# Attention with the values as the moving operand: one over the row sum applied to a token-major output that is transposed afterwards, and the statistics of the first projections taken after the third

## The chip, the core and the metric

The kernel runs on one core of a Trainium2 chip. The core has a matrix engine (TensorE, PE in the profile; its weight loads are the row PEld), VectorE (DVE), ScalarE (ACT), GpSimd (POOL) and SyncE (SP), which issues most DMAs. The engines run side by side, each through its own instructions in a fixed order, and wait for each other by semaphores. The metric is the device time of one execution in microseconds; the median of several runs counts.

## The reference, cut to what matters

A two-layer encoder over 1024 tokens of width 1024, float32. Layer 0 is a pair of recurrent mixers, layer 1 is softmax attention in chunks; each layer ends with an MLP and a gated embedding. The change lies in layer 1, whose attention is

```python
def chunk_band_attention(h, w_qkv, q_g, k_g, rel_bias):
    qkv = (h @ w_qkv).reshape(bsz, seq, 3, C_HEADS, C_HEAD_DIM)      # 16 heads x 64
    q = rmsnorm(qkv[:, :, 0], q_g) * (C_HEAD_DIM ** -0.5)
    k = rmsnorm(qkv[:, :, 1], k_g)
    v = qkv[:, :, 2]
    ...
    def one_chunk(c):                                                # CHUNK = 64, the chunk and 8 before it
        s = jnp.einsum('bqhd,bkhd->bhqk', q_c, k_b).astype(jnp.float32) + bias
        s = jnp.where(valid, s, -jnp.inf)
        prob = jax.nn.softmax(s, -1).astype(v.dtype)
        return jnp.einsum('bhqk,bkhd->bqhd', prob, v_b)
```

where h is the RMS-normalised residual, and the result goes through the output projection `attn_w_out`.

## The kernel before

**Staging.** Matrix products are made in two float32r parts, a rounded high part and the rest, so that one float32 product is three matmuls (high x high, high x low, low x high); where one operand isn't split, two. Layer 1's attention walks 16 steps s: 8 pairs of heads `pr` times two halves `hf` of the tokens. Four generators share PE: two `attn_lane`s, `attn_norms` and `attn_ins`. `Trunk.run` picks the next one to go on: it keeps a planned time `now`, which `mm` and `tr` move on by a planned length, and a yield with a name delays its generator by the figure for it in the table `LAT`; of those whose time has come, the first in the list goes on, so that the projections of `attn_ins` fill what the lanes leave. Behind that, the framework's scheduler sets each engine's final order and the semaphores, from the dependencies between tiles.

**Projections.** `attn_in` makes, for 128 tokens at a time, a group of 24 matmuls of 128x384 (q, k and v of a pair of heads) in a bank of the two-deep pool `dps`. ACT and DVE evacuate it to `qk` and `vs` with the scale `rscol`, one over the root mean square of the token. For the first pair of heads `rscol` is made by `row_stats` behind the first group: eight matmuls against ones over `accs`, which GpSimd sums in layer 0's tail (L1627), then a chain of small DVE operations (L375, L286 to L291). `load_qkv` brings the weights of the next pair: three pieces `wraw` by DMA, each split by ACT (L1824) and DVE (L1825). `attn_norm` transposes q and k (`dps<-ident,qk`) and normalises them.

**One job** (`attn_block`) is 256 queries, two groups of 128, of one head. For each group the scores of up to five blocks of 128 keys are made in the PSUM tiles `sn` (near keys) and `sf` (far keys); DVE adds the relative bias and takes the maximum; ACT takes the exponential into `pb` with its sum in `l` (L1967, L1970); DVE adds the sums and takes the reciprocal (L1972, L1973); ACT multiplies `pb` by it (L1974). Then PE transposes the blocks of `pb` into `pt`, ACT and DVE split them into `ptile` (L349, L350), and PE makes the output in `po`: the key block's values `vs` are stationary and the transposed probabilities of up to 256 queries move past. `vs` holds, in 128 columns, the high part of a head's 64 columns and the low part beside it, so half of `po`'s partitions hold the product with the one and half that with the other. After a head's second job ACT copies one half (L2015, `otmp`) and DVE adds the other (L2016, `y`). `y` is head-major, and after the second head it is written to DRAM for the output projection; for the last step it is split straight into `ylast`. `po` is one bank, shared by the two jobs of a head, and the next head waits until it is read.

The order that the change touches: a job's value product waits in the plan for that of the job before (`("pv", job - 1)`), and a step's projections for the step three before to be done (`("at", s - 3)`).

## Time and profile before

| | us |
|---|---|
| median of 3 runs (3086.08 to 3091.52) | 3089.84 |
| the profiled execution | 3089.73 |
| its span, first to last instruction | 3088.0 |
| the attention stage in it, 1691 to 2308 | 617 |
| PE busy in that stage | 567.78 |
| ACT busy in that stage | 433.73 |
| DVE busy in that stage | 427.33 |

The profile is of one execution. A row of a group gives the line, the engine and operation, out<-in by the program's names, the shape and count, the busy time, the mean length of one in ns, and the idle time of the engine ahead of it with what ended it. A row of a stretch gives its bounds, its length, and the busy time of each engine with its instructions, the granted clock of PE, the share of the DMA engines and GB/s. A row of the timeline gives start and length in us. Matmuls follow each other faster than one takes, so their pace is read from the starts.

### The profile page before, as it was taken

What the parts mean: (1) busy time and instruction counts of PE and PEld (TensorE: products, weight loads), DVE (VectorE), ACT (ScalarE), POOL (GpSimd) and SP (SyncE); (2) the same over time, 40 slices, a digit from 0 to 9 for tenths busy, and PEclk for the clock granted to TensorE, in tenths of its full rate; (3) what the DMA queues carried; (4) which work ended last, traced back from release to release, by engine and by line L of the source; (5) the groups of instructions that cost most, each with busy time, mean ns of one, the idle gap of its engine ahead of it and who ended that gap; (6) DMA issues with size and microseconds to landing.
All of it is one profiled execution on the core that took longest, in us unless ns stands there. A gap on an engine that the chain in (4) does not pass through costs nothing.

```text
span 3088.0 us, 47130 instructions
## 1 busy us (share of the span) xinstructions
PE 2979.5 (96%) x17288; PEld 2461.2 (80%) x17288; DVE 2232.1 (72%) x4518; ACT 1510.7 (49%) x2922; POOL 544.9 (18%) x978
## 2 busy tenths in 40 slices
PE   7999999999999999999999999989899999999999
PEld 5777778777777888888887988888788888888887
DVE  6656676657849788878867666766768888888762
ACT  4333443334427544444434577777756544544431
POOL 6533442443500000000015111100110000000002
PEclk9999999999999999999999999999999999999999
DMA  4211112211346434754424101100256444754432
GB/s 138 72 54 62 55 55 74 62 53 64 125 158 219 158 148 150 259 167 150 137 89 144 34 33 36 53 33 16 72 177 225 151 154 150 255 172 150 126 109 102
DMA packets 187639, 358.45 MB, mean 116 GB/s; under 512 B 45712, under 2 KB 47888, under 8 KB 187408
## 3 DMA queue, kind: packets, MB, share of 16 engines
q1 hardware_dynamic: 158608, 303.00, 29.6%
q10 hardware_dynamic: 28800, 52.44, 4.4%
q8 instruction: 136, 2.23, 0.3%
...
## 4 chain that ended last, share of the span: by engine, by line
PE 79%; DVE 10%; ACT 4%; DMA 3%; POOL 2%; issue 2%; SPq 0%; DVEq 0%; POOLq 0%; ACTq 0%
PE dps L177 66%; PE ch L177 2%; PE pm L177 2%; PE iz L177 1%; PE po L177 1%; PE tp L177 1%; DVE ptile L350 1%; PE pt L192 1%; DVE pb L1957 1%; PE sn L177 1%; POOL subt L415 1%; PE py L177 1%; DMA wraw<-in_w_qkv 1%; ACT pb L1970 1%; POOL sub L417 1%
## 5 line engine op out<-in xcount | busy, mean ns | idle before, releaser
L177 PE MATMUL dps<-r,act 128*128 128x512 f32 x3528 | 829.4, 392 | 0.0
L177 PEld LDWEIGHTS dps<-r,act 128*128 128x128 f32 x3528 | 662.0, 188 | 145.8
L177 PE MATMUL dps<-xg,whi 128*128 128x512 f32 x1280 | 434.0, 419 | 14.9 <-ACT xg L352 7.4
L1614 POOL TENSOR_TENSOR pn<-pn,prs 128x512 f32<-128x512 f32 x32 | 47.1, 1474 | 1543.1 <-ACT prs L386 1447.7
L177 PE MATMUL dps<-wq,act 128*128 128x384 f32 x1536 | 305.7, 345 | 6.4 <-DVE vs L1866 3.1
L177 PEld LDWEIGHTS dps<-xg,whi 128*128 128x128 f32 x1280 | 233.9, 195 | 67.9 <-issue 8.0
L177 PEld LDWEIGHTS dps<-wq,act 128*128 128x128 f32 x1536 | 266.6, 191 | 10.5 <-DVE vs L1866 4.9
L177 PE MATMUL dps<-xg,wlo 128*128 128x512 f32 x640 | 258.8, 405 | 1.3 <-DVE wlo L304 1.3
L177 PE MATMUL dps<-late,act 128*128 128x512 f32 x960 | 229.2, 392 | 0.0
L177 PEld LDWEIGHTS dps<-late,act 128*128 128x128 f32 x960 | 180.3, 188 | 39.7
L1271 ACT CAST act<-act 128x512 fp32r<-128x512 f32 (+1 forms) x223 | 137.6, 649 | 131.6 <-PE dps L177 67.5
L1384 DVE TENSOR_TENSOR late<-late,dps 128x512 f32<-128x512 f32 x224 | 152.4, 684 | 52.2 <-PE dps L177 45.8
L1271 ACT CAST act<-late 128x512 fp32r<-128x512 f32 x210 | 124.2, 617 | 133.2 <-PE dps L177 90.4
L177 PE MATMUL dps<-act 128*128 128x512 f32 x672 | 165.0, 392 | 0.0
L1272 DVE TENSOR_TENSOR act<-act 128x512 fp32r<-128x512 f32 (+1 forms) x223 | 154.8, 721 | 6.0 <-ACT act L1271 5.8
L177 PEld LDWEIGHTS dps<-act 128*128 128x128 f32 x672 | 126.1, 188 | 28.7
L1272 DVE TENSOR_TENSOR act<-late,act 128x512 fp32r<-128x512 f32 x210 | 141.5, 688 | 8.9 <-ACT act L1271 7.0
L177 PEld LDWEIGHTS dps<-xg,wlo 128*128 128x128 f32 x640 | 124.4, 194 | 29.2 <-DVE wlo L304 1.8
L303 ACT CAST whi<-wraw 128x1024 fp32r<-128x1024 f32 x78 | 81.9, 1050 | 122.0 <-PE dps L177 82.4
L1522 DVE TENSOR_TENSOR xw<-xw,dps 128x512 f32<-128x512 f32 x174 | 118.0, 683 | 31.5 <-PE dps L177 31.5
L177 PE MATMUL dps<-xw,act 128*128 128x512 f32 x576 | 139.6, 392 | 0.0
L1389 ACT ACTIVATE late<-late 128x512 f32<-128x512 f32 x128 | 80.3, 630 | 119.4 <-DVE late L1384 113.5
...
## 6 DMA issues: line engine op xcount, KB each, us to landing
...
```

What stands on the lines that cost most here:

```text
L177: return self.begin(self.nc.tensor.matmul(out, lhsT, rhs, start=start, stop=stop, skip_group_check=again))
L192: return self.begin(self.nc.tensor.transpose(out, in_, ident))
L303: nc.scalar.copy(hi, raw)
L350: nc.vector.tensor_tensor(dst[:, 1, sl], src, dst[:, 0, sl].bitcast(F32), op=ALU.subtract)
L415: E.tensor_tensor(o, X[:, 0:i, i:i + 1].broadcast_to((NP, i, n)), Bq[:, i:i + 1, i + 1:16].broadcast_to((NP, i, n)), op=ALU.mult)
L417: E.tensor_tensor(X[:, 0:i, i + 1:16], X[:, 0:i, i + 1:16], o, op=ALU.add)
L1271: A.copy(hi, s)
L1272: V.tensor_tensor(lo, s, hi.bitcast(F32), op=ALU.subtract)
L1384: V.tensor_tensor(r, t, u, op=ALU.add)
L1389: A.activation(t, t, AF.Relu)
L1522: V.tensor_tensor(x[n][:, hs[hf]], x[n][:, hs[hf]], ps, op=ALU.add)
L1614: G.tensor_tensor(pn, pn, prs[:, sl], op=ALU.mult)
```

## The change

Per group of 128 queries, the transposed probabilities (`ptile`) are now stationary and the values `vs` move past, so `po` is token-major: for a group, 128 tokens by the 64 columns of the high part and the 64 of the low. A job that made 12 matmuls (8 of 256 columns, 4 of 128; fewer near the start) makes 20 of 128. The pass L1974 over `pb` is gone; one over the sum is applied when a group's output is evacuated: ACT copies the high half times it into the token-major `y`, DVE adds the low half times it (L2021 and L2022 of the new kernel). After the second head's second job, and a new yield `attn_block4`, PE transposes the four token groups of `y` into a `pt` bank, and ACT copies that to the tile that goes to DRAM, or the split for `ylast` reads it. `l` gets eight buffers for four, since it is read later.

For the first pair of heads the first two projection groups go to the two `sn` banks and the third to a `dps` bank; `row_stats` runs behind the third, in a `pt` bank, and the three are evacuated after it.

In the table, `attn_block1` goes from 4.45 to 3.60 and `attn_block4` is new at 0.75.

```diff
--- before.py
+++ after.py
@@ -84,9 +84,10 @@
     "gdn_back4": 1.83,
     "attn_norm0": 0.24,
     "attn_block0": 0.97,
-    "attn_block1": 4.45,
+    "attn_block1": 3.60,
     "attn_block2": 0.43,
     "attn_block3": 0.94,
+    "attn_block4": 0.75,
     "qk": 11.25,
     "norm": 1.28,
     "end_front": 46.33,
@@ -363,11 +364,11 @@
             nc.scalar.activation(sq, src, AF.Square)
             nc.gpsimd.tensor_tensor(acc, acc, sq, op=ALU.add)
 
-    def row_stats(self, accs, out, scale=1.0 / D, eps=1e-6):
+    def row_stats(self, accs, out, scale=1.0 / D, eps=1e-6, bank=None):
 
         nc = self.nc
         nt = out.shape[-1]
-        ps = self.stat_bank()
+        ps = bank if bank is not None else self.stat_bank()
         for i in range(nt):
             self.mm(ps[:, i:i + 1], accs[i // 4][:, (i % 4) * P:(i % 4 + 1) * P], self.ones[:, 0:1],
                              start=True, stop=True)
@@ -1844,9 +1845,21 @@
         qk = wp.tile([P, 4, 256], F32, tag="qk", name="qk")
         vs = l1.tile([P, 4, 2, P], F32R, tag="vs", name="vs", bufs=4)
         kv["vs"] = kv["vs"] + [vs]
+        def scale(i, e, ps):
+            rc = self.rscol[:, i:i + 1]
+            A.activation(qk[:, e, :], ps[:, 0:2, :].rearrange("p a c -> p (a c)"), AF.Copy, scale=rc)
+            v3 = ps[:, 2, :].rearrange("p (h d) -> p h d", h=2)
+            vf = vs[:, e].rearrange("p h c -> p (h c)").rearrange("p (q d) -> p q d", d=64)
+            hi = vf[:, 0:4:3, :]
+            A.activation(hi, v3, AF.Copy, scale=rc)
+            V.scalar_tensor_tensor(vf[:, 1:3, :], v3, rc, hi.bitcast(F32), op0=ALU.mult, op1=ALU.subtract)
+        held = []
         for e in range(4):
             i = 4 * hf + e
-            ps = self.bank([P, 3, P])
+            if pr == 0 and i < 2:
+                ps = psm.tile([P, HB], F32, tag="sn", name="dps", bufs=2)[:, 0:3 * P].rearrange("p (a c) -> p a c", a=3)
+            else:
+                ps = self.bank([P, 3, P])
             ts = slice(i * P, i * P + P)
             for k in range(NK):
                 ks = slice(k * P, k * P + P)
@@ -1855,15 +1868,13 @@
                 self.mm(ps, xh, wl[:, :, ks], start=False, stop=False)
                 self.mm(ps, xl, wh[:, :, ks], start=False, stop=k == NK - 1)
                 yield 0
-            if pr == 0 and i == 0:
-                self.row_stats(self.accs, self.rscol)
-            rc = self.rscol[:, i:i + 1]
-            A.activation(qk[:, e, :], ps[:, 0:2, :].rearrange("p a c -> p (a c)"), AF.Copy, scale=rc)
-            v3 = ps[:, 2, :].rearrange("p (h d) -> p h d", h=2)
-            vf = vs[:, e].rearrange("p h c -> p (h c)").rearrange("p (q d) -> p q d", d=64)
-            hi = vf[:, 0:4:3, :]
-            A.activation(hi, v3, AF.Copy, scale=rc)
-            V.scalar_tensor_tensor(vf[:, 1:3, :], v3, rc, hi.bitcast(F32), op0=ALU.mult, op1=ALU.subtract)
+            held.append((i, e, ps))
+            if pr == 0 and i == 2:
+                self.row_stats(self.accs, self.rscol, bank=psm.tile([P, HB], F32, tag="pt", name="st", bufs=2))
+            if pr or i > 1:
+                for h in held:
+                    scale(*h)
+                held.clear()
             yield 0
         q4 = qk.rearrange("p i c -> p (i c)").rearrange("p (n d) -> p n d", d=64)
         ss = self.sm.tile([P, 16], F32, tag="ss1", name="ss1")
@@ -1914,7 +1925,6 @@
             t = st["toep"][h]
             G.tensor_scalar(t, t, rbl[:, 2 * pr + h:2 * pr + h + 1], None, op0=ALU.subtract)
             G.memset(t[0:64, 320:384], NEG)
-        hs = slice(64 * h, 64 * h + 64)
         Q, Ql, K, vs, toep = st["Q"], st["Ql"], st["K"], st["vs"], st["toep"][h]
 
         def score(ps, m, j0, n):
@@ -1956,7 +1966,7 @@
             S = pb[:, nf * P:(nf + nn) * P]
             V.tensor_tensor_reduce(S, pn[:, 0:nn * P], toep[:, (3 - nn) * P:], op0=ALU.add, op1=ALU.max,
                                    scale=1.0, scalar=NEG, accum_out=mx[:, 0:1])
-            l = sm.tile([P, 4], F32, tag="l", name="l", bufs=4)
+            l = sm.tile([P, 4], F32, tag="l", name="l", bufs=8)
             if nf:
                 pf = psm.tile([P, HB], F32, tag="sf", name="sf")
                 score(pf[:, 0:nf * P], m, f0, nf)
@@ -1971,8 +1981,7 @@
             if nf:
                 V.tensor_tensor(l[:, 0:1], l[:, 0:1], l[:, 1:2], op=ALU.add)
             V.reciprocal(l[:, 2:3], l[:, 0:1])
-            A.activation(pb[:, 0:(nf + nn) * P], pb[:, 0:(nf + nn) * P], AF.Copy, scale=l[:, 2:3])
-            probs.append((pb, f0))
+            probs.append((pb, f0, l[:, 2:3]))
             yield "attn_block0"
         yield "attn_block1"
 
@@ -1981,7 +1990,7 @@
             yield ("pv", job - 1)
         if blk == 0:
             st["po", h] = psm.tile([P, HB], F32, tag="o", name="po")
-        po = st["po", h][:, 256 * blk:256 * blk + 256]
+        po = st["po", h].rearrange("p (m c) -> p m c", m=4)[:, 2 * blk:2 * blk + 2]
         pts = []
         for b in range(bank + 1):
             pt = psm.tile([P, HB], F32, tag="pt", name="pt", bufs=2)
@@ -1990,7 +1999,7 @@
                     continue
                 for e in range(2):
                     if c0 <= 128 * e < c1:
-                        pb, f0 = probs[e]
+                        pb, f0, _ = probs[e]
                         self.tr(pt[:, o + 128 * e - c0:o + 128 * e - c0 + P],
                                             pb[:, (j - f0) * P:(j - f0 + 1) * P], self.ident)
             t = self.wp.tile([P, 2, HB], F32R, tag="ptile", name="ptile", bufs=3)
@@ -1998,31 +2007,33 @@
             pts.append(t)
             yield "attn_block2"
         yield "attn_block3"
-        nmm = 2 * len(segs)
-        q = 0
-        for j, c0, c1 in segs:
-            b, o, _, _ = place[j]
-            for part in range(2):
-                self.mm(po[:, c0:c1], vs[j // 4][:, j % 4, h, :], pts[b][:, part, o:o + c1 - c0],
-                                 start=q == 0, stop=q == nmm - 1)
-                q += 1
-        if blk == 1:
-            if h == 0:
-                st["y"] = l1.tile([P, HB], F32, tag="y", name="y", bufs=1)
-            y, po = st["y"], st["po", h]
-            oth = slice(64 * (1 - h), 64 * (1 - h) + 64)
-            tmp = l1.tile([P, HB], F32, tag="otmp", name="otmp", bufs=1)
-            A.copy(tmp[hs], po[oth])
-            V.tensor_tensor(y[hs], po[hs], tmp[hs], op=ALU.add)
-            if h == 1:
-                if s == 15:
-                    yield ("ylast", 0)
-                    self.split_scaled(self.ylast, y, None, slice(0, HB))
-                else:
-                    nc.sync.dma_start(out=self.yd[pr][hf], in_=y)
-                self.dump("y1", y, (pr, slice(None), slice(hf * HB, hf * HB + HB)))
-                self.mark(("at", s))
+        if h == 0 and blk == 0:
+            st["y"] = l1.tile([P, 4, 2, 64], F32, tag="y", name="y", bufs=1)
+        for e in range(2):
+            js = [j for j, c0, c1 in segs if c0 <= 128 * e < c1]
+            for j in js:
+                b, o, c0, _ = place[j]
+                o += 128 * e - c0
+                for part in range(2):
+                    self.mm(po[:, e, :], pts[b][:, part, o:o + P], vs[j // 4][:, j % 4, h, :],
+                            start=j == js[0] and part == 0, stop=j == js[-1] and part == 1)
+            y, rl = st["y"][:, 2 * blk + e, h, :], probs[e][2]
+            A.activation(y, po[:, e, 0:64], AF.Copy, scale=rl)
+            V.scalar_tensor_tensor(y, po[:, e, 64:128], rl, y, op0=ALU.mult, op1=ALU.add)
         self.mark(("pv", job))
+        if h == 1 and blk == 1:
+            yield "attn_block4"
+            pt = psm.tile([P, HB], F32, tag="pt", name="pt", bufs=2)
+            for e in range(4):
+                self.tr(pt[:, e * P:(e + 1) * P], st["y"][:, e].rearrange("p h d -> p (h d)"), self.ident)
+            if s == 15:
+                yield ("ylast", 0)
+                self.split_scaled(self.ylast, pt, None, slice(0, HB))
+            else:
+                yt = l1.tile([P, HB], F32, tag="otmp", name="yt", bufs=1)
+                A.copy(yt, pt)
+                nc.sync.dma_start(out=self.yd[pr][hf], in_=yt)
+            self.mark(("at", s))
```

What this makes of the order. First PE, in the middle of the stage: one job's value product before, with the transposes of `pb` around it. A row with waits names the engine whose semaphore it waits for.

```order
L177 MATMUL po<-ptile,vs 128x256 [waits Activation_49]
L192 MATMUL pt<-ident,pb 128x128 [waits DVE_49]
L192 MATMUL pt<-ident,pb 128x128
L177 MATMUL po<-ptile,vs 128x256 x3
L177 MATMUL po<-ptile,vs 128x256 [waits Activation_49]
L177 MATMUL po<-ptile,vs 128x256 [waits DVE_49]
L177 MATMUL po<-ptile,vs 128x256 x2
L192 MATMUL pt<-ident,pb 128x128 [waits PE_49]
L192 MATMUL pt<-ident,pb 128x128 x2
L177 MATMUL po<-ptile,vs 128x128 [waits Activation_49]
L177 MATMUL sn<-F_18446,F_18496 128x128 [waits DVE_49]
L177 MATMUL sn<-F_18446,Ql 128x128
```

In the new kernel, at a like place: the end of a first group's ten matmuls and a second group's ten.

```order
L178 MATMUL sn<-F_18642,Ql 128x128
L178 MATMUL sn<-F_18642,F_18663 128x256 [waits DVE_49]
L178 MATMUL sn<-F_18642,Ql 128x256
L178 MATMUL po<-vs,ptile 128x128 [waits DVE_49]
L193 MATMUL pt<-ident,pb 128x128 [waits PE_49]
L193 MATMUL pt<-ident,pb 128x128 x3
L178 MATMUL po<-vs,ptile 128x128 [waits DVE_49]
L178 MATMUL po<-vs,ptile 128x128 x9
L178 MATMUL sf<-F_17760,F_18228 128x128 [waits Activation_49]
L178 MATMUL sf<-F_17760,Ql 128x128
L178 MATMUL sf<-F_18215,F_18228 128x128
L178 MATMUL sf<-F_18215,Ql 128x128
```

The transposes that stood between the parts of one product now stand between the two groups, and the second group's ten matmuls follow a wait on DVE of their own, as the single matmul ahead, the last of the first group, has one.

Next DVE, at the start of layer 1: the weights of the second pair (L1825) and the chain of the statistics, before and now (L1826 and L376 in the new kernel). `ms` is the first operation of the chain.

```order
L353 TENSOR_SCALAR act<-x_12864,vecs,act 128x512 [waits Activation_49]
L1825 TENSOR_TENSOR wq_16248<-wraw,wq_16247 128x1024 [waits DMAHW6_49,PE_49,Activation_49]
L1825 TENSOR_TENSOR wq_16248<-wraw,wq_16247 128x1024 [waits DMAHW7_49,Activation_49]
L375 TENSOR_SCALAR ms<-dps 128x8 [waits PE_49]
L286 TENSOR_SCALAR rscol<-ms 128x8 [waits DVE_49]
L289 TENSOR_TENSOR rsw<-rscol 128x8 [waits DVE_49]
```

```order
L354 TENSOR_SCALAR act<-x_12864,vecs,act 128x512 [waits Activation_49]
L1826 TENSOR_TENSOR wq_16244<-wraw,wq_16243 128x1024 [waits DMAHW6_49,PE_49,Activation_49]
L1826 TENSOR_TENSOR wq_16244<-wraw,wq_16243 128x1024 [waits DMAHW7_49,Activation_49]
L1826 TENSOR_TENSOR wq_16244<-wraw,wq_16243 128x1024 [waits DMAHW2_49,Activation_49]
L376 TENSOR_SCALAR ms<-st 128x8 [waits PE_49]
L287 TENSOR_SCALAR rscol<-ms 128x8 [waits DVE_49]
L290 TENSOR_TENSOR rsw<-rscol 128x8 [waits DVE_49]
```

The third weight piece, which stood behind the statistics' chain, now stands ahead of it.

Last ACT, within the stage: the softmax of several jobs before, and at a like place now, where L1977 and L1980 are the exponentials and L2021 is the first half of a group's evacuation.

```order
L1967 ACTIVATE pb,l<-sf,mx 128x256 [waits DVE_49]
L1970 ACTIVATE pb,l<-pb,mx 128x384
L1974 ACTIVATE pb<-pb,l 128x640 [waits DVE_49,Activation_49]
L1861 ACTIVATE qk<-dps,rscol 128x256 [waits PE_49]
L1865 ACTIVATE vs<-dps,rscol 128x2x64
L1967 ACTIVATE pb,l<-sf,mx 128x256 [waits DVE_49]
L1970 ACTIVATE pb,l<-pb,mx 128x384
L349 COPY ptile<-pt 128x512 [waits PE_49] x2
L1974 ACTIVATE pb<-pb,l 128x640 [waits DVE_49,Activation_49]
L1861 ACTIVATE qk<-dps,rscol 128x256 [waits PE_49]
L1865 ACTIVATE vs<-dps,rscol 128x2x64
```

```order
L1854 ACTIVATE vs<-dps,rscol 128x2x64
L1977 ACTIVATE pb,l<-sf,mx 128x256 [waits DVE_49,Activation_49]
L1980 ACTIVATE pb,l<-pb,mx 128x384
L350 COPY ptile<-pt 128x512 [waits PE_49,Activation_49]
L2021 ACTIVATE y<-po,l 128x64 [waits PE_49]
L350 COPY ptile<-pt 128x384 [waits Activation_49]
L1850 ACTIVATE qk<-dps,rscol 128x256 [waits PE_49,Pool_49]
L1854 ACTIVATE vs<-dps,rscol 128x2x64
L1977 ACTIVATE pb,l<-sf,mx 128x256 [waits DVE_49,Activation_49]
L1980 ACTIVATE pb,l<-pb,mx 128x384
L2021 ACTIVATE y<-po,l 128x64 [waits PE_49]
```

The passes of L1974 are gone, and one or two evacuations of 128x64 stand where they stood, behind exponentials.

## The prediction

> **What bounds the kernel now.** I read the page first, then busy time by stretch, then the chain of waits in the stretches where TensorE (PE) is not full, then the waits by engine. The change lies in the attention stage, from 1691 to 2308 us of the span.
>
> ```profile
> span 3088.0 us, 47130 instructions
> PE 2979.5 (96%) x17288; PEld 2461.2 (80%) x17288; DVE 2232.1 (72%) x4518; ACT 1510.7 (49%) x2922; POOL 544.9 (18%) x978
> ...
> core 0: us, PE busy (x) PEld busy (x) DVE busy (x) ACT busy (x) POOL busy (x), PEclk, DMA share, GB/s
> 1691.00:2308.00 617.00, 567.78 (x3473) 527.18 (x3474) 427.33 (x1353) 433.73 (x1007) 78.68 (x79) 0.97 0.17 58
> 2005.50:2018.00 12.50, 8.89 (x57) 7.02 (x55) 9.37 (x41) 9.02 (x28) 1.04 (x1) 1.00 0.07 29
> 2021.00:2027.00 6.00, 4.98 (x36) 4.18 (x34) 4.09 (x11) 4.30 (x12) 0.00 (x0) 1.00 0.00 0
> 2045.00:2053.00 8.00, 6.17 (x40) 4.71 (x38) 6.48 (x19) 7.85 (x17) 1.04 (x1) 1.00 0.00 1
> 2003.00:2072.00 69.00, 62.39 (x404) 58.10 (x403) 48.26 (x162) 50.89 (x120) 7.12 (x8) 1.00 0.11 37
> ```
>
> The last row is one of eight like periods, a pair of heads each. PE is idle for 6.6 of its 69 us, and the three stretches above it hold 3.6 + 1.0 + 1.8 = 6.4 of them. There the projections have run out and PE waits for the softmax; elsewhere PE is full and every matmul added is paid in whole. Of the 72 value matmuls of the period, 24 + 9 + 9 = 42, or 58%, fall in the thin stretches (the same windows for the tile po alone):
>
> ```profile
> 2005.50:2018.00 12.50, 4.43 (x24) 3.47 (x24) 0.61 (x1) 0.14 (x1) 1.00 0.07 29
> 2021.00:2027.00 6.00, 1.70 (x9) 1.34 (x9) 0.00 (x0) 0.00 (x0) 1.00 0.00 0
> 2045.00:2053.00 8.00, 1.92 (x9) 1.33 (x9) 0.00 (x0) 0.00 (x0) 1.00 0.00 1
> 2003.00:2072.00 69.00, 12.93 (x72) 10.30 (x72) 2.75 (x4) 2.32 (x4) 1.00 0.11 37
> ```
>
> The chain of waits over 2009 to 2018, by line, says who sets the pace there: ACT, with the normalising pass L1974, which the change removes, second.
>
> ```profile
> by line: ACT pb L1970 28.2%; ACT pb L1974 15.7%; ACT ptile L349 11.4%; ACT pb L1967 10.1%; PE po L177 9.1%; PE pt L192 8.7%; DVE ptile L350 7.8%; issue 4.9%; DVE vs L1866 2.9%; DVE l L1972 1.9%; DVE l L1973 1.8%
> ```
>
> **The value product (A).** Before, a key block is stationary and up to 256 queries stream past; now 128 queries' probabilities are stationary and 128 columns of values stream. The columns streamed stay the same, the weight loads don't: 576 matmuls become 960 (per head 1+2+3+4+5+5+5+5 = 30 blocks, in two parts, 16 heads). The rows for the pace, and the counts before:
>
> ```profile
> 2013.72 0.90 PEld L177 LDWEIGHTS po<-ptile,vs 128*128 128x128 f32 x7
> ...
> 2004.97 0.22 PE L177 MATMUL sf<-F,F 128*128 128x128 f32 x1
> 2005.03 0.27 PE L177 MATMUL sf<-F,Ql 128*128 128x128 f32 x1
> 2005.14 0.28 PE L177 MATMUL sf<-F,F 128*128 128x128 f32 x1
> 2005.25 0.27 PE L177 MATMUL sf<-F,Ql 128*128 128x128 f32 x1
> 2005.36 0.39 PE L177 MATMUL dps<-wq,act 128*128 128x384 f32 x1
> ...
> 2003.96 0.82 PE L192 MATMUL pt<-ident,pb 128*128 128x128 f32 x6
> ...
> L177 PE MATMUL po<-ptile,vs 128*128 128x256 f32 x384 | 78.9, 313 | 13.9 <-ACT ptile L349 6.2 <-DVE ptile L350 6.1 <-DVE mx L1969 0.9
> L177 PE MATMUL po<-ptile,vs 128*128 128x128 f32 x192 | 34.2, 261 | 0.5 <-ACT ptile L349 0.4
> ```
>
> The seven loads of the first row belong to 256-wide matmuls: with the last one's 0.19 us taken off, (0.90 - 0.19) / 6 = 0.118 us each. The score matmuls are 128 wide with a new stationary each, as the new value matmuls will be: their starts are 0.06, then 0.11, 0.11, 0.11 apart. So half the columns cost nearly the same. Before: 384 x 0.118 + 192 x 0.0975 (a run of four) = 64.0 us. After: 960 x 0.111 = 106.6 us, or 97.7 if the first of each of the 178 runs in the new order takes 0.06. A is +34 to +43; I take +38.
>
> The Trainium skill ("TensorE: Matmul & The Clock Gate", section "Back-to-back issue gap") gives about 81 ns for a 128-wide load-and-matmul pair and 131 for a 512-wide one. By a straight line between them (an estimate from that page) the 256-wide pair is 98 ns and A is 960 x 0.081 - 384 x 0.098 - 192 x 0.081 = +25 us, which would make the forecast 13 us less. The rows here stand at 0.111 and 0.118, so the row decides.
>
> **The output transposes (B).** 64 of them, f32; six such in the row above take (0.82 - 0.27) / 5 = 0.11 us each: +7. Their 15 copies of 128x512 go to ACT, which loses more than that with L1974.
>
> **The early projections (C).** What the start loses now:
>
> ```profile
> 1692.09 1.86 PE L177 MATMUL dps<-ones,acc 128*128 128x1 f32 x8 [4.11 <-POOL acc L1627]
> 1694.60 5.81 PE L177 MATMUL dps<-wq,act 128*128 128x384 f32 x17 [0.64 <-DVE ms L375]
> 1696.60 1.05 ACT L1824 CAST wq<-wraw 128x1024 fp32r<-128x1024 f32 x1 [3.39 <-DMA wraw<-in_w_qkv]
> 1697.67 1.23 DVE L1825 TENSOR_TENSOR wq<-wraw,wq 128x1024 fp32r<-128x1024 f32 x1 [0.92 <-ACT wq L1824]
> ...
> 1694.60:1700.60 6.00, 6.00 (x19) 6.00 (x20) 3.33 (x12) 1.68 (x3) 1.64 (x3) 0.50 0.54 190
> 1700.60:1722.40 21.80, 21.80 (x128) 21.76 (x127) 6.87 (x20) 3.67 (x10) 3.13 (x3) 1.00 0.04 17
> ```
>
> PE stands 4.11 + 0.64 us, and then its granted clock is 0.50 for six us: 19 matmuls where 6.0 / (21.8 / 128) = 35 would fit, a loss of 2.8 us. Two more projections (48 x 0.17 = 8.2 us) cover the wait for acc, so 7.5 us can go. What is late next: the order of DVE, shown with the change, puts the statistics' chain behind the third weight piece, which ends at 1697.67 + 1.23 = 1698.9. The first three groups are evacuated after that, and the fifth needs the third's bank. PE's wait began at 1692.09 - 4.11 = 1688.0; two projections (8.2), half of the statistics (0.9) and the fourth group (24 x 0.17 = 4.1) end near 1701.2, so some idle comes back: nothing to 5.5 us, I take 2.5. C is -5, from -7.5 to -2.
>
> **The new wait (D).** The second excerpt of the order, above, shows, between the two query groups of a job, a wait on DVE in front of the second group's matmuls. It is for L2022, the evacuation of the group ahead out of the same po tile; 127 of the 128 groups wait so, where before 14 did, each with over 3.8 us of other matmuls between. Between the groups stands other PE work: by the rows' prices under 1.0 us in 32 places, over 1.5 in 88. Whatever is queued behind that matmul on PE, the other lane's transposes and the projections too, waits with it. The evacuation before:
>
> ```profile
> 2003.02 0.45 PE L177 MATMUL po<-ptile,vs 128*128 128x128 f32 x3
> 2003.59 0.58 ACT L2015 COPY otmp<-po 64x512 f32<-64x512 f32 x1
> 2005.44 0.68 DVE L2016 TENSOR_TENSOR y<-po,otmp 64x512 f32<-64x512 f32 x1
> ...
> 2015.64 0.54 PE L177 MATMUL po<-ptile,vs 128*128 128x128 f32 x3
> 2017.86 0.58 ACT L2015 COPY otmp<-po 64x512 f32<-64x512 f32 x1
> 2018.48 0.70 DVE L2016 TENSOR_TENSOR y<-po,otmp 64x512 f32<-64x512 f32 x1 [0.25 <-ACT otmp L2015]
> ...
> L449 ACT ACTIVATE Z<-iz,half 128x64 f32<-128x64 f32 x8 | 2.5, 311 | 11.8 <-PE iz L177 11.8
> L987 DVE SCALAR_TENSOR_TENSOR S<-S,ee,ch 128x64 f32<-128x64 f32 x24 | 6.7, 277 | 13.7 <-PE ch L177 13.6
> ```
>
> From the last matmul's end to the sum's end it took 2.65 and 3.0 us, of which 1.26 and 1.28 are the two operations and the rest queueing on ACT and DVE. Now they cost 0.31 + 0.28, with the hops 0.7 us; queueing adds 0 to 1.4. Summed over the 127 places, what the work between doesn't cover is 4 us at 0.7, 24 at 1.4, 57 at 2.1. I take the middle, +24.
>
> **What goes (E).** The waits of PE's weight loads over 1691 to 2308, in total:
>
> ```profile
> PEld po L177 <- ACT ptile L349: 12.0, 19, 1.3
> PEld pt L192 <- ACT pb L1974: 10.5, 11, 1.9
> PEld po L177 <- DVE ptile L350: 10.3, 18, 1.6
> PEld sf L177 <- ACT pb L1967: 6.7, 11, 1.6
> ```
>
> Without L1974 the transposes wait for the exponential alone. The planner moves them up by 0.85 us (4.45 to 3.60), but a 1.9 us wait outlives that little: -10. With a shorter ACT queue the 12.0 and 6.7 also shrink: -8 of them. E is -18, from 0 to -29.
>
> **What hides (F).** Of A + B = 45 us, 58% = 26 fall in stretches where PE is idle for 8 x 6.4 = 51 us. A burst of value matmuls hides where the other lane is in its softmax and not where its own lane waits for it: half, -13, from 0 to -26.
>
> **Sum.** 38 + 7 - 5 + 24 - 18 - 13 = +33 us. The profiled execution took 3089.73 us, 1.7 more than its span, and the median of the runs is 3089.84, so the sum goes on the median: **3123 us**; its own range, with one or two terms at an end, is 3100 to 3150.
>
> **Rivals.** *The chain decides and it gets faster.* If ACT sets the thin stretches, as the chain above says, new PE work there is free and only 42% of 45, 19 us, is paid; E reaches -29, C -8, D its floor of 4: 19 + 4 - 29 - 8 = -14, 3076 us. It decides if an evacuation is done within 1.0 us of its matmul. Against it: in the new ACT order L2021 stands behind the next job's exponentials. 0.22.
>
> *The evacuation becomes the bound.* With 2.1 us of it (57), nothing hidden and only the L1974 wait gone: 45 - 5 + 57 - 9 = +88, 3178 us. It decides once the ACT queue ahead of L2021 holds two exponentials most of the time. 0.10.
>
> *It evens out.* F at -26, D at 0.8 us (5): 45 - 5 + 5 - 18 - 26 = +1, 3091 us. 0.12.
>
> *The early projections don't come early.* If the weight piece eats all of C, the forecast is 3128; it is inside its range. A second idle PE at that place could also lower the clock again. The Trainium skill (the same page, "HAM oscillation — how this bites in real kernels") says that a gap over about 3.4 us brings PE back to half clock; the 0.50 after 4.11 us agrees, and by it a gap of 3.5 us instead of 2.5 would add about 3 us.
>
> **How the numbers follow.** Forecast 0.56, the others 0.22, 0.10, 0.12. Less than 0.2%, 6 us, can't be told from no change here. Faster 0.22, same 0.12, slower 0.56 + 0.10 = 0.66. The range runs from 3074, just under the first rival, to 3160, between the forecast and the second.
>
> **What would show it.** A: value matmuls 0.11 us apart in runs of eight to ten. C: no 4 us wait before the statistics, a clock of 1.00 there, a short wait for L1855 after the fourth group. D: waits of po for L2022 of 10 to 40 us together. E: no wait of pt longer than 1 us in total per period. Wrong if the thin stretches get shorter than 12.5 + 6 + 8 us, or if value matmuls come 0.06 us apart.

## The result, and the profile after

The changed kernel takes 3171.36 us (median of six runs, 3165.80 to 3183.23), the kernel before 3091.17 in the same comparison: a ratio of 1.0268, with an interval of 1.0243 to 1.0292. It is 80 us slower; the forecast was +33.

The page of the changed kernel's profiled execution (3172.39 us), span and busy time:

```profile
span 3170.6 us, 48239 instructions
PE 3050.7 (96%) x17736; PEld 2531.1 (80%) x17736; DVE 2237.9 (71%) x4614; ACT 1453.9 (46%) x2905; POOL 541.6 (17%) x978
...
L178 PE MATMUL po<-vs,ptile 128*128 128x128 f32 x960 | 147.7, 291 | 14.3 <-DVE y L2022 13.3
```

The line numbers are the new kernel's: L178 is `mm`, L193 the transpose, L2021 and L2022 the two halves of the evacuation, L350 and L351 the two halves of the probability tile. ACT has lost 57 us of work, PE has gained 71, and the value matmuls wait 13.3 us for L2022, which the kernel before did not have.

Busy time by stretch: the attention stage from its first projection to its last value matmul, and what follows it, in the kernel before. The columns are length, busy time and count by engine, granted clock, DMA share, GB/s.

```profile
1680.00:2307.00 627.00, 573.45 (x3504) 531.79 (x3503) 433.44 (x1359) 438.38 (x1014) 87.18 (x86) 0.97 0.18 60
2307.70:3088.00 780.30, 775.17 (x3394) 634.25 (x3392) 588.67 (x912) 349.43 (x578) 21.71 (x16) 1.00 0.46 159
```

The same two stretches in the changed kernel:

```profile
1682.00:2400.00 718.00, 658.24 (x4036) 614.77 (x4036) 450.63 (x1464) 381.76 (x1003) 85.58 (x86) 0.94 0.17 56
2399.80:3170.00 770.20, 760.15 (x3313) 620.75 (x3312) 582.42 (x903) 348.60 (x573) 21.68 (x16) 1.00 0.46 158
```

The stage grew by 90 us and what follows shrank by 10. Two things hide in that. The tail holds 3394 - 3313 = 81 matmuls fewer: dense work, 512 columns wide, 0.23 us each, which now runs inside the stage. That is 18.6 us moved (counted one by one in the trace it is 82 dense matmuls, less two transposes of the output that stand in the new tail), yet the tail is only about 9.5 shorter. And the clock fell from 0.97 to 0.94.

To see where the 90 us lie I split the stage's trace matmul by matmul. The time between the starts of two neighbours counts as work up to the pace of the first one's width (0.109 us for 128 columns, 0.118 for 256, 0.1735 for 384, 0.230 for 512). What is over is idle if the clock is full when the first one starts, and lost to the clock if it is at half (the stretched matmuls, and the little idle there). Going by the second one's start would move 5.5 us from idle to lost in the kernel before, 8.8 in the changed one and 2.2 in e6; the readings below hold either way. The table has the same split of every kernel tried. A row is of one profiled execution, up to 8 us from the median beside it, and a ratio is to the kernel before in the same comparison:

| kernel | median us, ratio | work | idle | lost to the clock | time at half clock | stage | tail |
|---|---|---|---|---|---|---|---|
| before | 3091.17 | 502.0 | 104.8 | 20.3 | 41.0 | 627.1 | 780.3 |
| changed | 3171.36, 1.0268 | 569.1 | 104.0 | 44.3 | 92.2 | 717.5 | 770.8 |
| e1 evacuation once a head | 3131.20, 1.0125 | 550.1 | 76.1 | 41.4 | 85.3 | 667.6 | 779.1 |
| e2 before, 128-wide values | 3119.79, 1.0087 | 545.5 | 76.8 | 35.6 | 75.1 | 658.0 | 775.5 |
| e3 before, no L1974 | 3082.10, 0.9971 | 496.7 | 93.2 | 21.1 | 44.4 | 611.0 | 784.6 |
| e4 before, early projections | 3084.41, 0.9983 | 510.1 | 102.2 | 13.3 | 27.3 | 625.6 | 772.7 |
| e5 e1, 256 columns streamed | 3107.09, 1.0049 | 554.5 | 80.5 | 6.1 | 13.7 | 641.1 | 780.8 |
| e6 evacuation once a job | 3103.30, 1.0040 | 543.2 | 72.7 | 10.0 | 20.5 | 626.0 | 784.7 |
| e7 changed, planner's price | 3165.15, 1.0233 | 567.8 | 80.0 | 61.2 | 119.5 | 709.1 | 770.0 |
| e8 before, two early projections | 3085.09, 0.9975 | 504.8 | 99.3 | 21.2 | 44.4 | 625.3 | 778.4 |
| e9 changed, 256 columns | 3163.96, 1.0217 | 570.2 | 112.8 | 18.2 | 41.0 | 701.2 | 774.1 |
| e10 e6, 256 columns | 3100.74, 1.0014 | 543.6 | 64.8 | 8.0 | 17.1 | 616.5 | 797.9 |
| e11 before, score pieces 256 wide | 3093.86, 1.0000 | 516.7 | 91.0 | 30.8 | 54.6 | 638.5 | 770.8 |
| e12 e4 and e11 | 3099.50, 1.0010 | 517.1 | 96.2 | 28.5 | 58.0 | 641.8 | 771.8 |
| e13 changed, work between groups | 3200.16, 1.0337 | 567.1 | 98.6 | 75.7 | 153.6 | 741.3 | 769.8 |
| e14 e6, due time 4.45 | 3116.42, 1.0066 | 541.6 | 75.5 | 19.6 | 41.0 | 636.6 | 794.5 |
| e15 e2, evacuation per group | 3179.58, 1.0284 | 555.1 | 105.8 | 55.3 | 102.4 | 716.2 | 768.9 |
| e16 e2, evacuation per job | 3116.30, 1.0076 | 540.3 | 77.9 | 31.7 | 58.0 | 649.9 | 781.9 |

Changed against before: work +67.1, of which 18.6 came over from the tail, so +48.5 is the change's own. Idle -0.8. Lost to the clock +24.0. The tail, 9.5 shorter where 18.6 left it, gives back 9.1. The stage's start, 1.8 us later, makes the sum: 48.5 - 0.8 + 24.0 + 9.1 + 1.8 = 82.6, the difference of the spans.

The weight loads' waits within the stage, after (us in total, times, longest):

```profile
PEld pt L193 <- DVE ptile L351: 19.3, 30, 1.8
PEld po L178 <- DVE y L2022: 18.5, 24, 2.7
PEld dps L178 <- DVE vs L1855: 9.0, 8, 4.9
PEld sf L178 <- ACT pb L1977: 5.9, 7, 1.3
```

The waits of before for L1974 (10.5) and for `ptile` at the value product (22.3 by its two halves) are gone from the head of the list. In their place stand 18.5 us for the evacuation and 19.3 of the transposes for the bank that L351 still reads: as much idle as before, under other names.

The start, by PE's timeline:

```profile
1687.37 9.11 PE L178 MATMUL dps<-wq,act 128*128 128x384 f32 x51 [1.05 <-ACT act L353]
1696.31 1.84 PE L178 MATMUL st<-ones,acc 128*128 128x1 f32 x16
1698.01 4.41 PE L178 MATMUL dps<-wq,act 128*128 128x384 f32 x24
1707.05 15.40 PE L178 MATMUL dps<-wq,act 128*128 128x384 f32 x72 [4.63 <-DVE vs L1855]
```

The 4.11 us in front of the statistics are gone, and 4.63 us for L1855 stand behind the fourth group instead.

The end of the stage. Before, PE's timeline has 97 dense matmuls left behind the last value product:

```profile
2307.27 0.44 PE L177 MATMUL po<-ptile,vs 128*128 128x128 f32 x3
2307.55 22.73 PE L177 MATMUL dps<-act,wq 128*128 128x512 f32 x97
```

After, 15 are left, and the last head's output must still be evacuated, transposed and copied:

```profile
2399.68 2.35 PE L178 MATMUL dps<-act,wq 128*128 128x512 f32 x9
2401.88 0.27 PE L193 MATMUL pt<-ident,y 128*128 128x128 f32 x1
2402.82 1.92 PE L178 MATMUL dps<-act,wq 128*128 128x512 f32 x6 [0.68 <-ACT act L350]
2409.53 15.77 PE L178 MATMUL dps<-act,late 128*128 128x512 f32 x53 [4.79 <-ACT late L1272]
```

PE stands bare for 0.68 + 4.79 us and runs at half clock from 2409.2 for 6.8 us, which loses another 3.4. Together that is 8.9 of the 9.1 us that the tail gives back: the cover for the end was spent in the stage.

### The profile page after: what moved, and what is told of

It is laid out like the page before. It is cut to its first block, busy times and chain, and to the rows that moved or that the text cites. A ratio compares the mean times of both kernels' runs of the same rounds, so it can differ in the third digit from the quotient of the medians.

```text
span 3170.6 us, 48239 instructions
## 1 busy us (share of the span) xinstructions
PE 3050.7 (96%) x17736; PEld 2531.1 (80%) x17736; DVE 2237.9 (71%) x4614; ACT 1453.9 (46%) x2905; POOL 541.6 (17%) x978
## 4 chain that ended last, share of the span: by engine, by line
PE 79%; DVE 10%; ACT 4%; DMA 3%; POOL 2%; issue 2%; SPq 0%; ACTq 0%; DVEq 0%; POOLq 0%
PE dps L178 65%; PE po L178 2%; PE ch L178 2%; PE pm L178 1%; PE iz L178 1%; PE sn L178 1%; PE pt L193 1%; PE tp L178 1%; DVE ptile L351 1%; DMA wraw<-in_w_qkv 1%; PE py L178 1%; DVE pb L1967 1%; DMA wraw<-in_w_out 1%; POOL subt L416 1%; POOL sub L418 1%
## 5 line engine op out<-in xcount | busy, mean ns | idle before, releaser
L178 PE MATMUL dps<-r,act 128*128 128x512 f32 x3528 | 829.1, 392 | 0.0
L178 PEld LDWEIGHTS dps<-r,act 128*128 128x128 f32 x3528 | 662.1, 188 | 145.8
L178 PE MATMUL dps<-xg,whi 128*128 128x512 f32 x1280 | 433.5, 419 | 14.3 <-ACT xg L353 7.4
L178 PE MATMUL dps<-wq,act 128*128 128x384 f32 x1536 | 308.5, 352 | 10.1 <-DVE vs L1855 7.0
L178 PEld LDWEIGHTS dps<-wq,act 128*128 128x128 f32 x1536 | 279.8, 199 | 14.0 <-DVE vs L1855 9.0
L178 PEld LDWEIGHTS dps<-xg,whi 128*128 128x128 f32 x1280 | 233.2, 195 | 67.2 <-issue 8.1
L178 PE MATMUL dps<-xg,wlo 128*128 128x512 f32 x640 | 258.5, 404 | 1.1 <-DVE wlo L305 1.1
L178 PE MATMUL dps<-late,act 128*128 128x512 f32 x960 | 229.2, 392 | 0.0
L178 PEld LDWEIGHTS dps<-late,act 128*128 128x128 f32 x960 | 180.3, 188 | 39.7
L178 PE MATMUL dps<-act 128*128 128x512 f32 x672 | 164.7, 392 | 0.0
L178 PE MATMUL po<-vs,ptile 128*128 128x128 f32 x960 | 147.7, 291 | 14.3 <-DVE y L2022 13.3
L178 PEld LDWEIGHTS po<-vs,ptile 128*128 128x128 f32 x960 | 136.5, 208 | 21.1 <-DVE y L2022 18.5
L178 PEld LDWEIGHTS dps<-act 128*128 128x128 f32 x672 | 126.2, 188 | 28.7
L178 PEld LDWEIGHTS dps<-xg,wlo 128*128 128x128 f32 x640 | 124.2, 194 | 29.0 <-DVE wlo L305 1.6
L1523 DVE TENSOR_TENSOR xw<-xw,dps 128x512 f32<-128x512 f32 x174 | 117.9, 682 | 32.1 <-PE dps L178 29.8
```

The costliest lines, as they stand in the source:

```text
L178: return self.begin(self.nc.tensor.matmul(out, lhsT, rhs, start=start, stop=stop, skip_group_check=again))
L1523: V.tensor_tensor(x[n][:, hs[hf]], x[n][:, hs[hf]], ps, op=ALU.add)
```

## The experiments

Two theories were set against each other first. T1: the new wait for L2022, with what it drags behind it, costs what goes beyond the weight loads. T2: the 128-wide matmuls, bound by their loads, do it all.

**e1: one evacuation for each head**, all four groups behind its second job, so that no wait stands inside a job.

```
-            y, rl = st["y"][:, 2 * blk + e, h, :], probs[e][2]
-            A.activation(y, po[:, e, 0:64], AF.Copy, scale=rl)
...
+        if blk == 1:
+            for g in range(4):
+                y, rl = st["y"][:, g, h, :], st["rl", h, g // 2][g % 2]
+                A.activation(y, po4[:, g, 0:64], AF.Copy, scale=rl)
...
```

> The changed kernel, with the four query groups of a head evacuated together after its second job: a group no longer waits for the evacuation of the one ahead, 18 waits on it stay and each has 3.8 us or more of other matmuls before it. Matmuls, passes and the early projections stay as in the change. Theory 1 (the waits on L2022, and the half clock that PE falls to behind them, are what the change costs beyond its weight loads): the 18.5 us of waits and most of the 50 us more at half clock go, 3171 falls to 3120 to 3140, and the time at half clock in the attention stage from 89 to about 40 us. Theory 2 (the 128-wide matmuls alone set the time and the clock, since PE streams only half of the time in them): 3160 to 3175, still over 75 us at half clock.

3131.20, 1.0125 (1.0111 to 1.0139): 40 us come back, in the range of T1. By the table 27.9 of the spans' 41.8 are idle, 2.9 clock, and 10.7 the cover at the end (19.0 less work in the stage, the tail only 8.3 longer). But the time at half clock stayed at 85 us, and T1 had made that a consequence of the waits. So the clock needed a cause of its own.

**e2: the kernel before with its 256-wide value matmuls cut into 128-wide ones**, term A alone.

```
-        for j, c0, c1 in segs:
...
+        for c in (0, P):
+            pieces = [(j, part) for j, c0, c1 in segs if c0 <= c < c1 for part in range(2)]
...
```

> The kernel before, with its value matmuls of 256 columns cut into two of 128: 960 instead of 576, the values stationary as before, no wait added, the pass L1974 kept. It is term A alone. Theory 1: 960 x 0.111 - 64 = +38 to +43 us of PE work, part of it hidden in thin stretches, 3111 to 3134, time at half clock near the 39 us of before. Theory 2: the same work and a clock that falls with it, 3140 to 3160, over 70 us at half clock.

3119.79, 1.0087 (1.0073 to 1.0100). Work rose by 43.5, of which 21 dense matmuls (4.8 us) came from the tail: A is +39. Idle fell by 28.0: the new matmuls fill that much of the thin stretches. And 15.3 more were lost to the clock, with no new wait at all. So the time is where T1 put it, and the 75.1 us at half clock are where T2 put them.

**e3: the kernel before without the pass L1974**, due time 3.60. It leaves out the division by the row sums.

```
-            A.activation(pb[:, 0:(nf + nn) * P], pb[:, 0:(nf + nn) * P], AF.Copy, scale=l[:, 2:3])
```

> The kernel before without the normalising pass L1974 (the output is left undivided by the row sums) and with the planner's 3.60 in place of 4.45: term E alone. If the pass is on the path as the chain in the thin stretches says: -10 to -29 us, 3062 to 3081. Rival: other waits take its place (the split of the transposes, DVE's queue), -5 us or less, 3086 to 3091.

3082.10, 0.9971 (0.9957 to 0.9986): -9, half of term E, and between the two ranges expected.

**e4: the kernel before with three early projections**, statistics behind the third (the change's edits of `row_stats` and the loop over e), and **e8**, the same with two:

```
-            if pr == 0 and i == 2:
+            if pr == 0 and i == 1:
...
-            if pr or i > 1:
+            if pr or i > 0:
```

> The kernel before with the early projections alone, the statistics behind the third group: term C alone. By the trace of the change a wait of 4.6 us for the evacuation after the fourth group takes the place of the 4.1 us wait for the sums, and the clock falls there all the same: 3089 to 3092, no difference that can be told. The forecast's own figure was -5, 3086.

> The kernel before with two early projections instead of three, statistics behind the second, everything else as before. The version with three early waited 4.6 us for the evacuation of its third group and gained 8 us against the kernel before in its call. If that wait was the rest of the price, 3076 to 3082; if the clock and the work behind it decide, 3083 to 3087.

3084.41 (0.9983, 0.9972 to 0.9995) and 3085.09 (0.9975, 0.9963 to 0.9988): -5 and -8 by the ratios. The forecast's C was -5; my expectation for e4, 3089 to 3092, was too pessimistic. Between the two there is no difference that these intervals show. But e8 doesn't say what the 4.6 us wait for L1855 is worth, since it didn't take it away: in its trace the statistics still run behind 71 of the first 72 projections, and PE then waits 4.58 us for the evacuation, against 4.40 in e4.

### The clock

The spells at half clock in these traces begin on a grid of 3.41 us (1972.3 and 2125.8 in the changed kernel are 45 steps of 3.413 apart) and last a multiple of it. The place ahead of 1972.3 in the changed kernel, by busy time:

```profile
1965.50:1968.90 3.40, 2.64 (x20) 2.44 (x21) 2.68 (x13) 1.35 (x5) 0.35 (x2) 1.00 0.00 0
1968.90:1972.30 3.40, 2.30 (x19) 1.91 (x17) 1.15 (x6) 2.27 (x9) 0.00 (x0) 0.99 0.02 5
1972.30:1986.00 13.70, 13.16 (x52) 12.48 (x53) 6.05 (x27) 5.09 (x18) 0.00 (x0) 0.50 0.00 1
1986.00:1989.40 3.40, 3.40 (x26) 3.21 (x24) 1.05 (x3) 1.80 (x5) 0.00 (x0) 1.00 0.00 0
```

and PE's timeline from there on:

```profile
1968.66 0.62 PE L193 MATMUL pt<-ident,pb 128*128 128x128 f32 x4
1969.03 0.31 PE L178 MATMUL sf<-F,F 128*128 128x128 f32 x1
1969.17 0.27 PE L178 MATMUL sf<-F,Ql 128*128 128x128 f32 x1
1969.33 0.55 PE L193 MATMUL pt<-ident,pb 128*128 128x128 f32 x3
1970.72 1.33 PE L178 MATMUL po<-vs,ptile 128*128 128x128 f32 x10 [0.85 <-DVE y L2022]
1972.84 0.69 PE L193 MATMUL pt<-ident,pb 128*128 128x128 f32 x2 [0.79 <-DVE ptile L351]
...
1979.50 2.23 PE L178 MATMUL po<-vs,ptile 128*128 128x128 f32 x10
1981.53 0.43 PE L193 MATMUL pt<-ident,y 128*128 128x128 f32 x1
1981.62 5.51 PE L178 MATMUL dps<-wq,act 128*128 128x384 f32 x19
```

Between 1968.9 and 1972.3 PE is busy for 2.30 us and idles for two short waits, 0.85 and part of 0.79. But all 17 matmuls that start there are 128 wide: 17 x 128 = 2176 columns, where dense work at 0.230 us for 512 streams 7600. Then the clock is 0.50 for 13.7 us. At half clock ten value matmuls take 2.2 us, so even without a break they stream only some 2000 columns in 3.41 us, and the clock comes back only once the nineteen 384-wide projections run.

I added up the columns of the matmuls that start in each such stretch, over the stages of all 18 kernels here but for their first and last 13 us or so, and looked at the clock of the next stretch:

| columns in a stretch of 3.41 us | at full clock: stretches, half clock next | at half clock: stretches, half clock next |
|---|---|---|
| under 1800 | 77, 76 | 44, 44 |
| 1800 to 2600 | 123, 71 | 78, 67 |
| 2600 to 3500 | 213, 15 | 92, 34 |
| over 3500 | 2609, 0 | 99, 0 |

That suggests a rule: the clock follows how much streamed in the stretch before, and a busy time made of 128-wide matmuls with a load each (128 columns in 0.111 us) counts half of one made of 256-wide ones (256 in 0.118). But PE's busy time sorts the stretches at full clock nearly as well, so it was put to a test. (The expectation of e5 below says "in all traces so far"; one spell of the changed kernel, at 2289.7, begins behind 3328 columns.)

The Trainium skill says, on the page "TensorE: Matmul & The Clock Gate", section "HAM oscillation — how this bites in real kernels", that no idle gap should be over about 3.4 us. The grid of 3.41 us agrees with that figure; the rule doesn't foresee the row above, where no gap was longer than 0.85 us.

**e5: e1 with 256 columns streamed** in three of four query groups. The second 128 land in the next group's place, before that group begins.

```
-                    self.mm(po[:, e, :], pts[b][:, part, o:o + P], vs[j // 4][:, j % 4, h, :],
...
+                    w = 2 if 2 * blk + e < 3 else 1
...
+                    self.mm(po4[:, 2 * blk + e:2 * blk + e + w, :], pts[b][:, part, o:o + P], v,
...
```

> The kernel with one evacuation per head, but in three of the four query groups every value matmul streams 256 columns (its own 128 values and 128 more, written into the next group's place before that group begins): the same number of matmuls and weight loads, about the same engine time (0.118 against 0.111 us each, 720 of them: +5 us), twice the columns. In all traces so far half clock begins in a stretch of 3.41 us right behind one in which fewer than about 2200 to 2800 columns streamed. Theory columns: what grants the clock is the columns streamed, and cutting the value matmuls to 128 columns made more stretches fall short; then the time at half clock in the stage falls from 85 us to under 55 and the time from 3131 to 3108 to 3124. Rival busy: what counts is the time the engine is busy with loads and matmuls, or the waits; then the time at half clock stays over 70 us and the time is 3130 to 3140.

**e9: the changed kernel with the same edit**, its waits left as they are.

> The changed kernel with its value matmuls streaming 256 columns in three of four query groups (128 of them into the next group's place, overwritten when that group begins); evacuations and waits as in the change. Theory: columns and waits are two separate prices. Then the time at half clock in the stage falls from 92 to under 40 us, the waits for L2022 stay at 12 us or more, and the time is 3171 less (92 - 40) x 0.45 = 23, so 3143 to 3155. Rival: the half clock comes from the waits; then it stays over 70 us and the time is 3165 to 3180.

The stage of e1, by busy time:

```profile
1682.00:2350.00 668.00, 632.56 (x3968) 599.99 (x3967) 446.05 (x1454) 382.25 (x994) 83.88 (x86) 0.94 0.18 58
```

and that of e5:

```profile
1682.00:2330.00 648.00, 613.86 (x3981) 578.56 (x3980) 448.93 (x1459) 383.49 (x998) 88.89 (x88) 0.99 0.18 60
```

In e5 the time at half clock fell from 85.3 to 13.7 us and the kernel by 24, to 3107.09 (1.0049, 1.0036 to 1.0062), a little more than expected: wider matmuls, as many loads, more engine work (+4.4), less time. In e9 it fell from 92.2 to 41.0, as expected, but the time only to 3163.96 (1.0217, 1.0204 to 1.0230), short of the expected 3143 to 3155: of 26 us of clock won back, 8.8 came back as idle, probably since PE now reaches its waits sooner. Columns and waits are two prices that overlap. The order of the other instructions shifted a little in both, so the runs make columns likely as what counts; they don't prove it.

**e11: the kernel before with its 128-wide score pieces streamed twice**, 256 wide, and **e12**, that with e4.

```
+                if e == 1:
+                    w = 2
+                    k = k.rearrange("p (e c) -> p e c", e=1).to_broadcast([P, 2, P])
...
```

> The kernel before with every 128-wide piece of a score product streamed 256 wide (the same key block twice, into a column block that a later piece overwrites or nobody reads): 192 query groups' pieces, 384 matmuls at +0.007 us, +3 us of engine time. Theory columns: the time at half clock in the stage falls from 41 us to 20 to 30 us (10 of the 41 are at the start, which has no scores), worth 5 to 10 us; 3083 to 3091. Rival: half clock there stays at 35 us or more, 3092 to 3097.

> The same with three projections early as well, which alone took 3084: 3075 to 3084 by the theory of the columns, 3084 to 3089 by its rival.

Misses: 3093.86 (1.0000, 0.9989 to 1.0011) and 3099.50 (1.0010, 1.0000 to 1.0019), with 54.6 and 58.0 us at half clock instead of fewer. The spells in e11 stand at 1872.6, 1944.3 and 2016.0, once for each of three pairs of heads; the kernel before has one near the first place (1874.7) and none at the other two. The new widths made the order of the instructions another, and it brought thin stretches of its own. The onsets still follow the table (392 to 2176 columns ahead of the spells of e11), but what columns added in the old order would buy these two runs don't show.

### The wait

**e6: both groups of a job evacuated behind the second.** 63 of the 127 waits are left, all between jobs.

```
+        for e in range(2):
             y, rl = st["y"][:, 2 * blk + e, h, :], probs[e][2]
```

> The changed kernel with both groups of a job evacuated after the second of them, so that no wait for an evacuation stands between the two groups of a job; 63 of the 127 waits remain, between jobs, where more other work lies. Theory places: the waits within a job, with under 1.5 us of other work between, carry the cost; 3128 to 3142, the waits for L2022's successor under 6 us in total. Rival number: each of the 127 waits costs alike, or the two evacuations one behind the other are as bad between jobs; 3145 to 3160.

3103.30 (1.0040, 1.0025 to 1.0056): 68 us come back with one line, and the time is below both ranges. Idle falls by 31.3 and the loss to the clock by 34.3. No wait for the evacuation is in the first eleven of its list, which begins:

```profile
PEld pt L193 <- DVE ptile L351: 9.7, 13, 1.3
PEld dps L193 <- DVE vs L1855: 7.1, 4, 2.2
PEld dps L178 <- DVE vs L1855: 6.2, 4, 3.7
```

The bare waits alone don't add up to this. Of the 13.3 us for which the changed kernel's PE stands idle for L2022, 6.1 are 15 waits inside jobs and 7.2 are five between jobs; e6 keeps a hand-over between jobs and has 0.3 us of such waits left in all. Much of what it wins are waits further on, such as those of the transposes for L351 (19.3 to 9.7 us by the lists), and the clock.

It is more than e1 won by taking out more waits. What e1 keeps are 13.7 to 17.1 us at half clock once for each pair of heads (1871.7, 1946.8, 2021.9, 2100.4), with runs of 15 and 20 value matmuls in them; why its order has that place and e6's hasn't I did not test.

**e7: the changed kernel, the planner told what a value matmul takes.**

```
+                    self.now += 0.058
```

> The changed kernel with the planner told that a value matmul takes 0.058 us more than it assumes (0.111 in place of 0.053). Theory: the waits come from where the program order puts the second group, right behind the first, whatever the planner thinks of its length; 3160 to 3180, waits for the evacuation 12 us or more. Rival: the planner's clock runs ahead of the chip by 0.058 x 960 = 56 us over the stage, and that is why other work is spent too early and the waits stand bare; 3125 to 3150.

3165.15 (1.0233, 1.0219 to 1.0246), in the range of the theory, but not for its reason: the waits for the evacuation fell to 5.8 us, and idle by 24.0. The half clock took 16.9 of it back (44.3 to 61.2).

**e13: the changed kernel with other work allowed between the two groups of a job.**

```
+            if e == 0:
+                yield "attn_block5"
```

> The changed kernel with all its 128 evacuations where they are, but the planner may put other work between the two query groups of a job (due 1.4 us behind the first). Theory: it is the bare wait within the job that costs; covered, the time falls to 3100 to 3125, with waits for the evacuation under 6 us and under 45 us at half clock in the stage. Rival: the hand-over of the bank 127 times, or the order of the evacuations on ACT and DVE, costs by itself; 3140 to 3175.

A miss: 3200.16 (1.0337, 1.0306 to 1.0367), slower than the change. Its list of waits:

```profile
PEld po L179 <- DVE y L2023: 20.2, 18, 3.0
PEld pt L194 <- DVE ptile L352: 12.7, 19, 1.4
```

It lies above both ranges. The wait was not covered, it grew, and 153.6 us ran at half clock. Each job's chain has a step more now, which may be why. So this doesn't tell the wait from the hand-over.

**e10: e6 with the 256 columns of e5**, and **e14: e6 with the transposes' due time back at 4.45.**

> Evacuation once for each job, and 256 columns streamed in three of four groups. The kernel with the evacuation for each job alone took 3103 with 20 us at half clock in the stage. Columns: what is left at half clock goes to under 12 us, which saves 4, and the wider stream costs up to 5: 3098 to 3106. With neither price left, the rest against the kernel before is the weight loads and transposes (+45) less what hides of them (-30) and less the early projections (-5): +10, 3103.

> Evacuation per job, with the transposes' due time back at 4.45 us in place of 3.60. If the due time has no part in the change's loss, 3097 to 3110 (3103 with 3.60). If the earlier due time brings PE to its transposes before their exponentials are done, below 3097; if it is needed now that the pass is gone, 3112 or more.

e10 took 3100.74 (1.0014, 1.0002 to 1.0025), a time as expected, though half clock fell only from 20.5 to 17.1 us and not under 12: the change without the hand-over inside the job all but equals the kernel before. e14 took 3116.42 (1.0066, 1.0048 to 1.0083): the earlier due time is worth 8 us by the ratios, 13 by the medians, and no part of the loss.

**e15 and e16: the hand-over alone**, put into e2, which has nothing else of the change. e15 evacuates after each query group, e16 the same 128 pieces, two behind each job.

```
         for c in (0, P):
...
+            cs = slice(256 * blk + c, 256 * blk + c + P)
+            A.copy(tmp[hs, cs], whole[oth, cs])
+            V.tensor_tensor(y[hs, cs], whole[hs, cs], tmp[hs, cs], op=ALU.add)
```

> The kernel before with its value matmuls cut to 128 columns (3120 alone) and its evacuation, the same sum of two halves, made after each query group instead of once per head: 128 evacuations of 64x128 on ACT and DVE instead of 32 of 64x512, and the wait within the job. Nothing else of the change. Theory hand-over: 127 waits in the same place as in the changed kernel cost about what they cost there (68 us): 3160 to 3200, with waits for the evacuation over 12 us. Rival: the cost belongs to the changed kernel's other parts; 3120 to 3145.

> The same with the 128 evacuations made two by two, behind the second group of each job: as many operations on ACT and DVE, no wait within the job. Theory hand-over: 3110 to 3135, near the 3120 of one evacuation per head. Rival (the number of evacuations costs, not the wait): as e15, within 10 us.

3179.58 (1.0284, 1.0264 to 1.0304) against 3116.30 (1.0076, 1.0061 to 1.0091). The same matmuls, copies and sums in number and size, and 63 us between them: the hand-over inside the job is what costs, and the mere number of evacuations costs nothing that shows (e2, with a quarter as many, took 3119.79). The head of e15's waits:

```profile
PEld po L177 <- DVE y L2014: 17.4, 24, 1.6
PEld pt L192 <- DVE ptile L350: 11.8, 18, 1.5
PEld sf L177 <- ACT pb L1967: 10.9, 11, 2.3
```

against, in e16,

```profile
PEld po L177 <- DVE y L2015: 2.6, 4, 1.5
```

and e15's stage by busy time, where length and clock read like the changed kernel's:

```profile
1682.00:2400.00 718.00, 651.30 (x3945) 605.21 (x3945) 464.33 (x1462) 459.42 (x1115) 90.25 (x88) 0.93 0.17 55
```

Of the 59.5 us between the spans of e15 and e16, 27.9 are idle and 23.6 clock. No run gave the second group a bank of its own with the evacuation left inside the job. So it is shown that the evacuation inside the job costs this much, but not how much of it is the wait for the bank and how much the evacuation's place in the order of ACT and DVE.

## Why the prediction was wrong

It had the direction, and waits for L2022 within its 10 to 40 us, and was 47 us short, above its range of 3074 to 3160. The step that failed is D: the hand-over inside the job was priced at its own bare waits alone, with nothing for the waits that follow from them and nothing for the clock.

- **A and B, +45: right.** A alone measured +39 in e2, and A and B together +48.5 in the changed kernel. Its ten value matmuls at 2398.57 take 1.23 us, with the last one's 0.22 off 0.112 us each:

```profile
2398.57 1.23 PE L178 MATMUL po<-vs,ptile 128*128 128x128 f32 x10
```

The 81 ns of the Trainium skill ("TensorE: Matmul & The Clock Gate", section "Back-to-back issue gap") would have been too low here.

- **C, -5: right alone** (-5 and -8). In the changed kernel the stretch up to 1735 is 52.5 us long from the stage's start, against 54.3, with the same 216 projections begun, so some -2; the wait for L1855 that the prediction put at 2.5 us took 4.63, and brought 6.8 us at half clock (from 1706.0) in place of the 10.2 that the start had before. The prediction reads that half clock as following the gap of 4.11 us; by the record of the clock it begins at 1690.3, only 2.3 us into the gap, behind a step of the grid in which eight columns streamed.
- **E and F, -31 together: right as a sum, wrong in the split.** Without bare waits idle falls by 28.7 (e1) to 32.1 (e6). F alone gives 28 (e2), not 13: a burst of value matmuls fills thin stretches wherever its lane stands. There was also more to fill than the prediction read from busy time: 104.8 us of idle by the matmuls' starts, not 51. E alone gives 9 (e3), not 18, and adds little to F: they draw on the same idle time. Its sign, no more than 1 us of waits of `pt` in a period, failed: the 19.3 us for L351 are 2.4 in each of eight. And that e2 took 27 us more, near 38 - 13 = 25, is luck: 15 us more were hidden, and 15 lost to the clock.
- **D, +24: the step that failed.** The waits that it summed are there, and they are not longer than it said: 18.5 us by the weight loads, 13.3 as idle time of PE. But the hand-over inside the job costs 68 us in the change (e6) and 63 without the rest of the change (e15 against e16). Of that, 31 and 28 are idle, more than the bare waits, since other waits go with them: by the lists, e6 also cuts those of the transposes for L351 (19.3 to 9.7) and those of the scores for the exponentials (5.9 to 1.6). Another 34 and 24 are lost to the clock.
- **The evacuation is also longer than D took it.** "I take the middle" was one that ends 1.4 us behind its group's last matmul. From the trace of the changed kernel, L2022 ends 1.95 us (median of 128) behind the start of that matmul, so 1.73 behind its end. At the place shown above ACT is why: when the group's last matmul (1968.60) is done, near 1968.8, L2021 stands behind three exponentials,

```profile
1968.58 0.60 ACT L1980 ACTIVATE pb<-pb,mx 128x384 f32<-128x384 f32 x1
1969.08 0.19 ACT L1980 ACTIVATION_READ_ACCUMULATOR pb<-pb,mx 128x1 f32 x1
...
1970.05 0.29 ACT L2021 ACTIVATE y<-po,l 128x64 f32<-128x64 f32 x1
```

so the bank is handed over only at 1970.7. Elsewhere it is DVE, as between two jobs where PE idles for 1.12 us:

```profile
1932.82 0.31 ACT L2021 ACTIVATE y<-po,l 128x64 f32<-128x64 f32 x1
...
1933.01 0.42 DVE L1975 TENSOR_REDUCE mx<-sf 128x1 f32<-128x256 f32 x1
1933.46 0.74 DVE L1913 SCALAR_TENSOR_TENSOR F<-dps,vecs,F 64x512 fp32r<-64x512 f32 x1
1934.24 0.28 DVE L2022 SCALAR_TENSOR_TENSOR y<-po,l,y 128x64 f32<-128x64 f32 x1
```

Over the 128 evacuations, the mean delay beyond the shortest one is 0.53 us in front of L2021 and 0.63 between L2021 and L2022. The prediction looked for the queue on ACT; DVE's is as long.
- **The clock was missing from the sum.** The prediction priced half clock at the start of the stage alone. Everywhere else a wait was counted at its own length, and a 128-wide matmul at its pace at full clock; e2 alone lost 15.3 us there. And the wait inside a job falls where PE streams little anyway, among 128-wide matmuls, and the stretch behind it runs at half speed. In all that is +24.0 us in the changed kernel, of which e6 takes away all and more (44.3 to 10.0) and e9 most by columns alone (to 18.2).
- **The end of the stage** was put at nothing, and cost 9.1 us.

By the table the spans differ by 48.5 (A, B) - 32 (E and F, with C's idle) + 31 (idle of the hand-over) + 24 (clock) + 9 (the end) + 2 (the later start) = 82.5. The split makes these add up, so the sum itself is no proof; that the hand-over costs what it does rests on e6 and on e15 against e16. The rival that the evacuation becomes the bound came nearest (3178), by a sum that differs: it had nothing hidden and no clock. Its condition, two exponentials ahead of L2021 most of the time, doesn't hold, since L2021 starts 0.65 us (median) behind the start of the group's last matmul. So its nearness is luck.
